# The gate's matrix product over two token groups by seven products, with sums made by accumulating transfers

## Chip, cores and metric

One core of one Trainium2 chip runs the whole program. The time is the device time of one execution in microseconds, the median over runs. All data are f32; the large matmuls split each f32 operand into a rounded part and a rest and add three products of them ("three passes").

## The reference, cut to what matters

```python
mix = jnp.concatenate([y_ssd, y_sc], axis=-1) @ w_out      # 2048 tokens x 2048 @ 2048 x 1024
x = x + rmsnorm(mix, norm_post)
gate = jax.nn.sigmoid(x @ w_ple_gate)                      # 2048 x 1024 @ 1024 x 1024
return x + gate * (p_i @ w_ple_proj)
```

Ahead of these lines stand a normalised input projection, a state space scan and a short convolution; the change leaves them alone but for one scale factor.

## The kernel before

Everything is held transposed: 128 partitions are 128 features, the free dimension is tokens. Tokens come in four groups of 512 (`tg` 0 to 3, `TG` = 512), features in eight tiles of 128 (`d` or `k`, `KD` = 8), so that a tile is 128x512 f32, 256 KB. The input projection (to about 1190 us) already uses a seven product form (`Wino`, line 242): a 2x2 block product by 7 block products instead of 8, with sums of weight halves and of input halves. After the scan come the two stages concerned here, from about 1322 us to the end.

`out_proj(t)` (line 1042) treats token groups t and t+1 together. The half of the output projection that belongs to the convolution was made earlier, beside the scan, and lies in DRAM as `part_d`. A *unit* is one output tile of one group: 24 matmuls (8 k, three passes), into one bank of a PSUM pair (`pss`, 3 pairs of banks; `psm` holds 2 single banks). VectorE adds `part` from PSUM (L1060), ScalarE squares the sum (L1065), VectorE adds the squares up (L1066). There are 32 such units, numbered 0 to 31.

`norm(tg)` (line 1069) sums the squares over partitions by a product with ones (L1072), takes the root (L1074) and the reciprocal over 128x512 (L1075). `residual` (line 1077) multiplies by norm and column (L1081) and adds the input x, loaded as `xres` (L1082). `operands` splits the result for the matmuls (`split_act`, L203 a ScalarE cast, L204 a VectorE difference).

`gate(t)` (line 1089) has again 32 units of 24 matmuls (tiles `mg`), 768 in all; then tanh (L1104), plus one times the projected embedding `pe` (L1105), half of that plus x2 (L1106), and the store. The embeddings' projection `ple_d` is made at the start of the kernel (lines 393 to 402).

Weights come through `Weights` (line 110): pieces of 128x512 in one sequence, loaded to `raw` (9 buffers), cast (L138) and differenced (L139) into one of six slots. `W.next(held)` keeps the slots filled ahead of the matmuls. In `gate` and `out_proj` four pieces are held while both groups use them.

Steps that are not matmuls are hung on units by `after(unit, ...)`, run once the matmuls of that unit are issued. A scheduler then orders each engine's instructions by readiness and by this order; for instance four `mg` matmuls stand ahead of the last `mo` unit in the trace. All transfers are issued on SyncE's queue. `Loads` (line 746) is a pool of three buffers for loads of tile pairs (512 KB).

Of the kernel before, what the change touches and what calls it, by code (L numbers as in the profile page):

```python
# [15 lines left out]
P = 128  # L16
# [39 lines left out]

AHEAD, LATER = (0, 1), (2, 3)
# [3 lines left out]
def hybrid_kernel(ctx: ExitStack, tc: tile.TileContext, xT, pT, w_t, w_dt, w_o, w_g, w_p, cols_d, cst_d, outT):  # L61
# [19 lines left out]
    acs_d = [dram.tile([NH, TB], F32, name=f"acs_d{b}") for b in range(NB)]  # L81

# [24 lines left out]
    def col(i):  # L107
        return cols[:, i:i + 1]
# [253 lines left out]
    with ExitStack() as st:  # L362
# [9 lines left out]
        def first_input():  # L372
# [373 lines left out]
    class Loads:  # L746
# [5 lines left out]
        def begin(self, kind, *at):  # L752
# [3 lines left out]
            if kind in ("mraw", "gn"):  # L756
                b, o = divmod(at[0] * TG, TB)
            if kind == "gn":
                src = grs_d[b][:, o:o + TG].partition_broadcast(P)
            else:  # L760
                if kind == "mraw":
                    k = at[1]
                    src = yz_d[b][k:k + 2, :, o:o + TG] if k < KD else ysc_d[b][k - KD:k - KD + 2, :, o:o + TG]
                elif kind == "part":
                    src = part_d[at[0]][at[1]:at[1] + 2]
                else:
                    src = xT[at[1]:at[1] + 2, :, at[0] * TG:(at[0] + 1) * TG]
                src = src.rearrange("k p t -> p k t")
# [267 lines left out]
    with ExitStack() as st:  # L1036
        pp = st.enter_context(tc.tile_pool(name="pp", bufs=2))
        L3 = Loads(st, "pl3", 3)

        x2s_, ssq_, rs_, sp_ = {}, {}, {}, {}  # L1040

        def out_proj(t):

            for tg in (t, t + 1):
                x2s_[tg] = [None] * KD
                ssq_[tg] = pp.tile([P, TG], F32, tag="ssq", name=f"ssq2_{tg}")
            for dp in range(0, KD, 2):
                sp = []
                for tg in (t, t + 1):
                    x2, ssq = x2s_[tg], ssq_[tg]  # L1050
                    ps = pss.tile([P, 2, TG], F32, tag="ssd", name=f"mo_{tg}_{dp}")
                    pt = L3.get("part", tg, dp)
                    for i in range(2):
                        for q in range(2):
                            if tg == t:
                                sp.append(W.next(len(sp)))
                            mm3([(ps[:, i, :], sp[2 * i + q], acts_o[tg])], 4 * q, 4, KD)
                        d = dp + i
                        x2[d] = pp.tile([P, TG], F32, tag="x2", name=f"x2_{tg}_{d}", bufs=NG * KD)
                        V.tensor_tensor(x2[d], ps[:, i, :], pt[:, i, :], ALU.add)  # L1060
                        if d == 0:
                            S.activation(ssq, x2[d], AF.Square)
                        else:
                            sq = pp.tile([P, TG], F32, tag="sq2", name=f"sq2_{tg}_{d}")
                            S.activation(sq, x2[d], AF.Square)  # L1065
                            V.tensor_tensor(ssq, ssq, sq, ALU.add)  # L1066
                        yield

        def norm(tg):

            ps = mm_bank(f"pn2_{tg}")
            TE.matmul(ps, ones_d, ssq_[tg], start=True, stop=True)  # L1072
            rs = rs_[tg] = pp.tile([P, TG], F32, tag="rs2", name=f"rs2_{tg}")
            S.activation(rs, ps, AF.Sqrt, bias=epsc[:, 0:1])  # L1074
            V.reciprocal(rs, rs)  # L1075

        def residual(tg, d):

            x2, xk = x2s_[tg], L3.get("xres", tg, d)
            for i in range(2):  # L1080
                V.scalar_tensor_tensor(x2[d + i], x2[d + i], col(C_POST + d + i), rs_[tg], ALU.mult, ALU.mult)  # L1081
                V.tensor_tensor(x2[d + i], x2[d + i], xk[:, i, :], ALU.add)  # L1082

        def operands(tg, d):

            for i in range(2):
                sp_.setdefault(tg, []).append(split_act(x2s_[tg][d + i], f"x2s_{tg}_{d + i}", FIRST[2 * (tg % 2) + d // 4]))

        def gate(t):

            for dp in range(0, KD, 2):
                sp = []
                for tg in (t, t + 1):
                    banks = pss.tile([P, 2, TG], F32, tag="ssd", name=f"mg_{tg}_{dp}")
                    for i in range(2):
                        d, ts_, ps = dp + i, slice(tg * TG, (tg + 1) * TG), banks[:, i, :]
                        pe = pp.tile([P, TG], F32, tag="pe", name=f"pe_{tg}_{d}")
                        nc.sync.dma_start(pe, ple_d[tg * TG // TB][d, :, tg * TG % TB:tg * TG % TB + TG])
                        for q in range(2):
                            if tg == t:  # L1100
                                sp.append(W.next(len(sp)))
                            mm3([(ps, sp[2 * i + q], sp_[tg])], 4 * q, 4, KD)
                        th = pp.tile([P, TG], F32, tag="gth", name=f"gth_{tg}_{d}")
                        S.activation(th, ps, AF.Tanh, scale=0.5)  # L1104
                        V.scalar_tensor_tensor(th, th, 1.0, pe, ALU.add, ALU.mult)  # L1105
                        V.scalar_tensor_tensor(th, th, 0.5, x2s_[tg][d], ALU.mult, ALU.add)  # L1106
                        nc.sync.dma_start(outT[d, :, ts_], th)
                        yield

# [6 lines left out]
        def second(tg, at_norm, at_res, at_ops):  # L1116

            after(at_norm, lambda: norm(tg))
            for n, u in enumerate(at_res):
                after(u - 1, lambda d=2 * n: L3.begin("xres", tg, d))  # L1120
                after(u, lambda d=2 * n: residual(tg, d))
            for n, u in enumerate(at_ops):
                after(u, lambda d=2 * n: operands(tg, d))
# [6 lines left out]
        mixes_at(1, -1, -1, 0, 1)  # L1130
        mixes_at(2, 12, 13, 14, 14)
# [8 lines left out]
        for stage in (out_proj, gate):  # L1140
            for t in range(0, NG, 2):
                for _ in stage(t):
                    for step in plan.get(u, ()):
                        step()
                    u += 1

# [61 lines left out]
```

## Time and profile before

| | |
|---|---|
| median of 3 runs | 1699.23 us (1698.92 to 1703.21) |
| profiled execution | 1696.41 us, span 1694.7 us |
| PE, weight load, DVE, ACT, POOL busy | 98%, 80%, 74%, 46%, 3% |
| mean granted TensorE clock | 0.996 |
| transfers | 262.27 MB, 155 GB/s over the span, 46.4% of 16 engines on the one hardware queue |
| output projection (`mo`) | 1322.6 to 1511.9 us |
| gate (`mg`) | 1505.2 to 1689.2 us |

PE is TensorE, DVE VectorE, ACT ScalarE, POOL GpSimd, SP SyncE. The profile gives a group of instructions as line, engine, operation, out<-in by the program's names, and idle time by what ended it. "Landing" of a transfer is the time from its issue to its completion.

### The profile page before, as it was taken

What the parts mean: (1) busy time and instruction counts of PE and PEld (TensorE: products, weight loads), DVE (VectorE), ACT (ScalarE), POOL (GpSimd) and SP (SyncE); (2) the same over time, 40 slices, a digit from 0 to 9 for tenths busy, and PEclk for the clock granted to TensorE, in tenths of its full rate; (3) what the DMA queues carried; (4) which work ended last, traced back from release to release, by engine and by line L of the source; (5) the groups of instructions that cost most, each with busy time, mean ns of one, the idle gap of its engine ahead of it and who ended that gap; (6) DMA issues with size and microseconds to landing.
All of it is one profiled execution on the core that took longest, in us unless ns stands there. A gap on an engine that the chain in (4) does not pass through costs nothing.

```text
span 1694.7 us, 22635 instructions
## 1 busy us (share of the span) xinstructions
PE 1658.7 (98%) x8324; PEld 1351.9 (80%) x8324; DVE 1255.4 (74%) x1843; ACT 783.5 (46%) x1408; POOL 45.6 (3%) x79
## 2 busy tenths in 40 slices
PE   7999999999999999999999999999999899999998
PEld 5788888888888888888888888778777677788886
DVE  7997777988669867677777685689678748878632
ACT  7763444434337434343444353666575324252421
POOL 0000000000000100100000000000000000000000
PEclk9999999999999999999999999999999999999999
DMA  9462221773226322222222237789887735636422
GB/s 303 162 211 70 97 96 61 257 251 120 69 68 213 130 80 95 78 76 68 106 82 102 73 117 239 245 277 278 261 314 242 243 100 168 197 102 211 149 95 87
DMA packets 122691, 262.27 MB, mean 155 GB/s; under 512 B 17098, under 2 KB 19658, under 8 KB 121556
## 3 DMA queue, kind: packets, MB, share of 16 engines
q1 hardware_dynamic: 122580, 260.83, 46.4%
q8 instruction: 65, 1.06, 0.2%
q14 instruction: 46, 0.38, 0.1%
HBM read 192.45 MB, written 68.33 MB: 154 GB/s over the span
## 4 chain that ended last, share of the span: by engine, by line
PE 85%; DMA 6%; DVE 6%; ACT 2%; issue 1%; SPq 0%; DVEq 0%; ACTq 0%
PE mg L214 10%; PE mo L214 8%; PE os L826 6%; PE py L967 1%; PE A_xs1X L310 1%; PE A_gc6X L310 1%; PE A_gc7X L310 1%; PE A_gb6X L310 1%; PE A_z3X L310 1%; PE A_xs3X L310 1%; PE A_gc5X L310 1%; PE A_z2X L310 1%; PE A_xs2X L310 1%; PE A_gb4X L310 1%; PE A_gc4X L310 1%; PE A_gc3X L310 1%
## 5 line engine op out<-in xcount | busy, mean ns | idle before, releaser
L826 PE MATMUL os<-act_m,ws_os 128*128 128x512 f32 x768 | 186.0, 396 | 2.4 <-ACT po L830 1.7
L214 PE MATMUL mo<-act_m,ws_o 128*128 128x512 f32 x768 | 180.9, 396 | 4.3 <-DVE x L1060 4.3
L214 PEld LDWEIGHTS mo<-act_m,ws_o 128*128 128x128 f32 x768 | 144.1, 189 | 42.1 <-issue 6.1
L214 PE MATMUL mg<-act_x2s,ws_g 128*128 128x512 f32 x768 | 176.8, 391 | 0.7 <-ACT gth L1104 0.7
L826 PEld LDWEIGHTS os<-act_m,ws_os 128*128 128x128 f32 x768 | 141.2, 188 | 37.6 <-issue 6.6
L214 PEld LDWEIGHTS mg<-act_x2s,ws_g 128*128 128x128 f32 x768 | 143.0, 188 | 34.2 <-ACT gth L1104 4.4
L139 DVE TENSOR_TENSOR ws_A_gb<-wr_A_gb,ws_A_gb 128x512 fp32r<-128x512 f32 x96 | 65.8, 686 | 33.0 <-ACT ws_A_gb L138 32.9
L138 ACT CAST ws_A_gc<-wr_A_gc 128x512 fp32r<-128x512 f32 x96 | 59.7, 622 | 57.7 <-PE A_gc5X L310 8.3
L138 ACT CAST ws_A_gb<-wr_A_gb 128x512 fp32r<-128x512 f32 x96 | 59.7, 621 | 51.6 <-PE A_cb0Y L310 4.3
L604 DVE SCALAR_TENSOR_TENSOR xo<-ux,cols,xo 128x1024 f32<-128x1024 f32 x60 | 76.7, 1280 | 6.7 <-ACT xo L600 5.6
L939 ACT ACTIVATE m<-m,adt 128x128 f32<-128x128 f32 x256 | 77.5, 391 | 0.6 <-DMA m<-acs_d 0.5
L139 DVE TENSOR_TENSOR ws_A_gc<-wr_A_gc,ws_A_gc 128x512 fp32r<-128x512 f32 x96 | 66.0, 687 | 14.1 <-ACT ws_A_gc L138 12.8
L1105 DVE SCALAR_TENSOR_TENSOR gth<-gth,pe 128x512 f32<-128x512 f32 x32 | 22.1, 691 | 70.5 <-ACT gth L1104 70.4
L1104 ACT ACTIVATE gth<-mg 128x512 f32<-128x512 f32 x32 | 19.1, 598 | 103.7 <-PE mg L214 103.6
L214 PE MATMUL A_ple<-act_p,ws_p 128*128 128x512 f32 x192 | 48.2, 409 | 9.0 <-ACT ws_p L138 8.1
L942 DVE SCALAR_TENSOR_TENSOR m<-m,gsb 128x1024 f32<-128x1024 f32 x32 | 39.6, 1246 | 19.1 <-ACT m L939 16.8
L214 PEld LDWEIGHTS A_ple<-act_p,ws_p 128*128 128x128 f32 x192 | 37.4, 196 | 18.7 <-ACT ws_p L138 9.0
L139 DVE TENSOR_TENSOR ws_A_z<-wr_A_z,ws_A_z 128x512 fp32r<-128x512 f32 x48 | 32.9, 685 | 25.2 <-ACT ws_A_z L138 25.2
L203 ACT CAST act_m<-mraw 128x512 fp32r<-128x512 f32 x64 | 38.1, 621 | 28.9 <-DVE mraw L785 15.8
L138 ACT CAST ws_A_xs<-wr_A_xs 128x512 fp32r<-128x512 f32 x48 | 29.9, 623 | 44.3 <-issue 11.6
L138 ACT CAST ws_A_z<-wr_A_z 128x512 fp32r<-128x512 f32 x48 | 29.9, 623 | 41.9 <-DVE wr_A_z L187 8.6
L1060 DVE TENSOR_TENSOR x<-mo,part 128x512 f32<-128x512 f32 x32 | 22.0, 686 | 29.3 <-PE mo L214 29.3
(499 smaller groups left out, 3597.7 us busy)
## 6 DMA issues: line engine op xcount, KB each, us to landing
wr_A_gc<-in_w_t_dram SPq DMA_DIRECT2D x64, 256.0 KB, 2.5
wr_A_gb<-in_w_t_dram SPq DMA_DIRECT2D x64, 256.0 KB, 2.8
m<-acs_d SPq DMA_DIRECT2D x32, 512.0 KB, 7.7
ple_d<-A_pe SPq DMA_DIRECT2D x32, 256.0 KB, 5.1
wr_A_xs<-in_w_t_dram SPq DMA_DIRECT2D x32, 256.0 KB, 2.6
ysc_d<-vs SPq DMA_DIRECT2D x16, 512.0 KB, 2.7
wr_A_z<-in_w_t_dram SPq DMA_DIRECT2D x32, 256.0 KB, 3.0
xs_d<-xo SPq DMA_DIRECT2D x16, 512.0 KB, 4.0
```

The source lines that it names most:

```text
L138: S.copy(sp[:, 0, :kn, :], raw[:, :kn, :])
L139: V.tensor_tensor(sp[:, 1, :kn, :], raw[:, :kn, :], sp[:, 0, :kn, :].bitcast(F32), ALU.subtract)
L203: S.copy(a[:, 0, :], src)
L214: TE.matmul(out, sp[:, a, (k0 + k) % 4, :], act[k0 + k][:, b, :], start=k0 + k == 0 and q == 0, stop=k0 + k == n - 1 and q == 2)
L310: TE.matmul(out, sp[:, a, k % 4, :], t[:, b, ts_], start=p in OPENS and k == 0 and q == 0, stop=k == nk - 1 and q == 2, skip_group_check=True)
L604: V.scalar_tensor_tensor(o, u[:, q:q + TB], col(w0 + q), o, ALU.mult, ALU.add)
L826: TE.matmul(ps, sp[:, a, k, :], acts_o[tg][KD + kk][:, b_, :], start=kk == 0 and n == 0, stop=kk == KD - 1 and n == 2)
L939: S.activation(m[:, c, :], m[:, c, :], AF.Exp, bias=nacs[b][:, h, c:c + 1])
L942: V.scalar_tensor_tensor(mf, mf, 1.0, s["gsb"][gr], ALU.min, ALU.mult)
L1060: V.tensor_tensor(x2[d], ps[:, i, :], pt[:, i, :], ALU.add)
L1104: S.activation(th, ps, AF.Tanh, scale=0.5)
L1105: V.scalar_tensor_tensor(th, th, 1.0, pe, ALU.add, ALU.mult)
```

## The change

The gate's product is rewritten as a 2x2 block product: rows are the two halves of the output features (tiles 0 to 3 and 4 to 7), the inner dimension is the two halves of the input features, columns are token groups t and t+1. Seven products p, each of four output tiles n and four k tiles: 12 matmuls for each (p, n). A gate unit is now 12 matmuls; there are 28 for t = 0 (units 32 to 59) and 28 for t = 2 (units 60 to 87). Each has a weight piece of its own. Products 1, 6, 7 and 4 accumulate in bank X of their tile, 5 and 3 in another, 2 in a third; three of them (1, 5, 6) are copied out half-way (`kept`), and a finished tile is such a copy plus a bank (for product 4 the bank alone).

Four sums of weight halves per tile n are formed on VectorE during the output projection and stored to `sg_d` (`gate_sums`), then loaded as pieces. Operand sums are made on VectorE in place (`operand`: three for product 6, one for product 7).

Three additions move from VectorE to transfers that add into SBUF, issued by GpSimd: the stored half `part_d` into the copied bank (16 of 512 KB), the residual x (16 of 512 KB), and, for all but the last four tiles, x2 into the gated embedding (28 of 256 KB). For this last addition x2 is stored (`kept`, 16 stores of 512 KB, three or four units after the residual's transfer), since `operand` overwrites it. An output store stands three units after its accumulating transfer.

The norm takes four single-column products, root and reciprocal over 128x4, and spreads the result by a diagonal and a second product. The factor 0.5 of the gate moves to the embeddings' projection (`S.mul`, same instruction count).

```diff
+GORDER = (1, 2, 6, 5, 3, 7, 4)
+GATES = ([(p, n) for p in (1, 2, 6) for n in range(4)]
+         + [(p, n) for h in (0, 2) for p in (5, 3) for n in (h, h + 1)]
+         + [(p, n) for p in (7, 4) for n in range(4)])
...
+    def gate_piece(p, n):
+        if p in (1, 2, 4):
+            return w_g[n + 4 * int(p == 4), :, 4 * int(p != 1):4 * int(p != 1) + 4, :]
+        return sg_d[n][{5: 0, 6: 1, 7: 2, 3: 3}[p]]
...
-        seq += [direct(w_g[d, :, 4 * q:4 * q + 4, :], f"g{t}_{d}_{q}", praw) for d in range(KD) for q in (0, 1)]
+        seq += [direct(gate_piece(p, n), f"g{t}_{p}_{n}", praw) for p, n in GATES]
...
-                        S.copy(pe, ps)
+                        S.mul(pe, ps, 0.5)
...
-                        V.tensor_tensor(x2[d], ps[:, i, :], pt[:, i, :], ALU.add)
+                        S.copy(x[:, i, :], ps[:, i, :])
+                        if i == 1:
+                            G.dma_start(x, rows(part_d[tg][dp:dp + 2]), accum_op=ALU.add)
+                            unit = 8 * t + 2 * dp + 2 * (tg - t) + i
+                            lag = 4 if unit == 31 else 2
+                            after(unit + lag, lambda tg=tg, d=dp: squares(tg, d))
+                            after(unit + lag + 1, lambda tg=tg, d=dp: squares(tg, d + 1))
...
+            def sums():
+                ssq = ssq_[tg]
+                ps = mm_bank(f"pn2_{tg}")
+                for c in range(TG // P):
+                    TE.matmul(ps[:, c:c + 1], ssq[:, c * P:(c + 1) * P], ones_d[:, 0:1], start=True, stop=True)
+                q = const.tile([P, TG // P], F32, tag="rq2", name=f"rq2_{tg}")
+                S.activation(q, ps[:, 0:TG // P], AF.Sqrt, bias=epsc[:, 0:1])
+                V.reciprocal(q, q)
+                V.tensor_tensor(ssq.rearrange("p (c t) -> p c t", t=P), ident.unsqueeze(1).to_broadcast([P, TG // P, P]),
+                                q.unsqueeze(2).to_broadcast([P, TG // P, P]), ALU.mult)
+
+            def spread():
+                ps = mm_bank(f"prs2_{tg}")
+                TE.matmul(ps, ones_d, ssq_[tg], start=True, stop=True)
+                rs = rs_[tg] = pp.tile([P, TG], F32, tag="rs2", name=f"rs2_{tg}")
+                S.mul(rs, ps, float(D))
...
-                V.tensor_tensor(x2[d + i], x2[d + i], xk[:, i, :], ALU.add)
+            G.dma_start(x2s_[tg][d // 2], rows(xT[d:d + 2, :, tg * TG:(tg + 1) * TG]), accum_op=ALU.add)
+
+        def kept(tg, d):
+            nc.sync.dma_start(rows(x2_d[tg][d:d + 2]), x2s_[tg][d // 2])
...
+            a, b, c, d = w
+            V.tensor_tensor(d, c, d, ALU.add)
+            V.tensor_tensor(c, c, a, ALU.subtract)
+            V.tensor_tensor(a, a, d, ALU.subtract)
+            V.tensor_tensor(b, b, a, ALU.add)
...
+            if p == 6:
+                src = tmp(f"t2_{t}{k}")
+                V.tensor_tensor(b11, b12, b11, ALU.subtract)
+                V.tensor_tensor(src, b11, b22, ALU.subtract)
+                V.tensor_tensor(b21, b21, src, ALU.add)
+            elif p == 7:
+                src = b12
+                V.tensor_tensor(b12, b12, b22, ALU.subtract)
+            else:
+                src = {1: b11, 2: b21, 5: b11, 3: b22, 4: b21}[p]
...
+                V.scalar_tensor_tensor(th, th, 1.0, L.get("pe", tg, d - d % 2)[:, d % 2, :], ALU.add, ALU.mult)
+                store = lambda: nc.sync.dma_start(outT[d, :, tg * TG:(tg + 1) * TG], th)
+                if last and p == 4:
+                    V.tensor_tensor(th, th, L.get("x2", tg, d - d % 2)[:, d % 2, :], ALU.add)
+                    store()
+                else:
+                    G.dma_start(th, x2_d[tg][d], accum_op=ALU.add)
+                    after(unit + 3, store)
...
+                out, sp = bank[BANK[p], n], W.next()
+                for k in range(4):
+                    for q, (a, b) in enumerate(PASSES):
+                        TE.matmul(out, sp[:, a, k, :], ops_[t, p][k][:, b, :], start=p in OPENS and k == 0 and q == 0,
+                                  stop=k == 3 and q == 2, skip_group_check=True)
+                if p in (1, 5, 6):
+                    keep[p, n] = tmp(f"kp_{t}_{p}{n}")
+                    S.copy(keep[p, n], out)
+                else:
+                    finish(p, *at(p, n), out, keep.get(({2: 1, 3: 6, 7: 5, 4: 0}[p], n)), unit)
...
-        second(0, 16, (19, 20, 21, 22), (29, 29, 30, 30))
-        second(1, 18, (24, 25, 26, 27), (31, 31, 32, 32))
-        second(2, 32, (35, 36, 37, 38), (45, 45, 46, 46))
-        second(3, 34, (40, 41, 42, 43), (47, 47, 48, 48))
+        second(0, 17, (19, 20, 21, 22), 3)
+        second(1, 19, (23, 24, 25, 26), 3)
+        operands_at(0, 29, 30)
+        operands_at(1, 30, 31)
+        operands_at(2, 32, 33, 34, 35)
+        second(2, 33, (37, 39, 41, 43), 4)
+        operands_at(3, 36, 37)
+        second(3, 38, (45, 47, 49, 51), 4)
...
```

More of the change, by code (lines that the diff above doesn't have):

```diff
@@ L81, in hybrid_kernel @@
     acs_d = [dram.tile([NH, TB], F32, name=f"acs_d{b}") for b in range(NB)]
+    sg_d = [dram.tile([4, P, 4, P], F32, name=f"sg_d{n}") for n in range(KD // 2)]
+    x2_d = [dram.tile([KD, P, TG], F32, name=f"x2_d{g}") for g in range(NG)]
     cols = const.tile([P, NCOL], F32, name="cols")
@@ L755, in begin @@
             t = self.ready[(kind, *at)] = self.pool.tile([P, 2, TG], F32, tag="ld", name="_".join(map(str, (kind, *at))))
-            if kind in ("mraw", "gn"):
-                b, o = divmod(at[0] * TG, TB)
+            b, o = divmod(at[0] * TG, TB)
             if kind == "gn":
@@ L763, in begin @@
                     src = yz_d[b][k:k + 2, :, o:o + TG] if k < KD else ysc_d[b][k - KD:k - KD + 2, :, o:o + TG]
-                elif kind == "part":
-                    src = part_d[at[0]][at[1]:at[1] + 2]
+                elif kind == "pe":
+                    src = ple_d[b][at[1]:at[1] + 2, :, o:o + TG]
                 else:
-                    src = xT[at[1]:at[1] + 2, :, at[0] * TG:(at[0] + 1) * TG]
+                    src = x2_d[at[0]][at[1]:at[1] + 2]
                 src = src.rearrange("k p t -> p k t")
@@ L1037, in hybrid_kernel, with after, tmp, x2 @@
         pp = st.enter_context(tc.tile_pool(name="pp", bufs=2))
-        L3 = Loads(st, "pl3", 3)
-        x2s_, ssq_, rs_, sp_ = {}, {}, {}, {}
+        x2s_, ssq_, rs_, ops_ = {}, {}, {}, {}
+        plan = {}
+        def after(unit, *steps):
+            plan.setdefault(unit, []).extend(steps)
+        def tmp(name):
+            return pp.tile([P, TG], F32, tag="kp", name=name, bufs=11)
+        def x2(tg, d):
+            return x2s_[tg][d // 2][:, d % 2, :]
+        def rows(a):
+            return a.rearrange("k p t -> p k t")
+        def squares(tg, d):
+            ssq = ssq_[tg]
+            if d == 0:
+                S.activation(ssq, x2(tg, d), AF.Square)
+            else:
+                sq = pp.tile([P, TG], F32, tag="sq2", name=f"sq2_{tg}_{d}")
+                S.activation(sq, x2(tg, d), AF.Square)
+                V.tensor_tensor(ssq, ssq, sq, ALU.add)
         def out_proj(t):
             for tg in (t, t + 1):
-                x2s_[tg] = [None] * KD
+                x2s_[tg] = []
                 ssq_[tg] = pp.tile([P, TG], F32, tag="ssq", name=f"ssq2_{tg}")
@@ L1057, in out_proj @@
                             mm3([(ps[:, i, :], sp[2 * i + q], acts_o[tg])], 4 * q, 4, KD)
[L1058 to L1066, printed above, removed]
@@ new lines, in out_proj, with norm @@
+                        yield
+        def norm(tg, unit):
+            def sums():
+                ssq = ssq_[tg]
+                ps = mm_bank(f"pn2_{tg}")
[11 more added lines that the diff above has]
+                S.mul(rs, ps, float(D))
+            after(unit, sums)
+            after(unit + 1, spread)
@@ L1077, in residual @@
         def residual(tg, d):
-            x2, xk = x2s_[tg], L3.get("xres", tg, d)
             for i in range(2):
[L1081 to L1087, printed above, removed]
-        def gate(t):
[L1091 to L1108, printed above, removed]
@@ L1111, in hybrid_kernel @@
-        plan = {}
-        def after(unit, *steps):
-            plan.setdefault(unit, []).extend(steps)
-        def second(tg, at_norm, at_res, at_ops):
-            after(at_norm, lambda: norm(tg))
+                V.scalar_tensor_tensor(x2(tg, d + i), x2(tg, d + i), col(C_POST + d + i), rs_[tg], ALU.mult, ALU.mult)
+            G.dma_start(x2s_[tg][d // 2], rows(xT[d:d + 2, :, tg * TG:(tg + 1) * TG]), accum_op=ALU.add)
+        def kept(tg, d):
+            nc.sync.dma_start(rows(x2_d[tg][d:d + 2]), x2s_[tg][d // 2])
@@ L1119, in second, with operands_at @@
+        def second(tg, at_norm, at_res, lag):
+            norm(tg, at_norm)
             for n, u in enumerate(at_res):
-                after(u - 1, lambda d=2 * n: L3.begin("xres", tg, d))
                 after(u, lambda d=2 * n: residual(tg, d))
-            for n, u in enumerate(at_ops):
-                after(u, lambda d=2 * n: operands(tg, d))
+                after(u + lag, lambda d=2 * n: kept(tg, d))
+        def operands_at(g, *units):
+            for k in range(4):
+                after(units[k * len(units) // 4], lambda k=k: operand(g, k))
@@ L1145, in hybrid_kernel @@
                     u += 1
+        for v in sorted(plan):
+            if v >= u:
+                for step in plan[v]:
+                    step()
 _OUTS = [((KD, P, T), 'float32')]
```

68 lines of the change are left out of this document (60 added, 8 removed).

## The prediction

> **What bounds the kernel now.** I read the summary of the page first (busy shares), then the chain that ended last, then the stretch around the change (output projection and gate) by the chain in order of time, by windows and by engine timelines.
>
> ```profile
> span 1694.7 us, 22635 instructions
> PE 1658.7 (98%) x8324; PEld 1351.9 (80%) x8324; DVE 1255.4 (74%) x1843; ACT 783.5 (46%) x1408; POOL 45.6 (3%) x79
> PE 85%; DMA 6%; DVE 6%; ACT 2%; issue 1%; SPq 0%; DVEq 0%; ACTq 0%
> ```
>
> TensorE is busy 98% of the span and carries 85% of the chain: a matmul removed is worth its own pitch as long as nothing else takes its place. The end of the chain in order of time (start, length, what):
>
> ```profile
> 1505.37 0.91 PE mg L214 x4
> 1506.28 5.65 PE mo L214 x24
> 1511.93 4.54 PE mg L214 x20
> 1516.46 0.86 PE pn L1072 x2
> 1517.32 10.89 PE mg L214 x48
> 1528.22 0.86 PE pn L1072 x2
> 1529.08 153.69 PE mg L214 x672
> 1682.79 0.61 ACT gth L1104
> 1683.43 5.75 PE mg L214 x24
> 1689.20 0.61 ACT gth L1104
> 1689.84 0.70 DVE gth L1105
> 1690.56 0.69 DVE gth L1106
> ```
>
> The gate's 768 matmuls (mg) take 0.91+4.54+10.89+153.69+5.75 = 175.8 us, 0.229 us each, with one gap of 0.6 us. Who keeps TensorE waiting from 1320 us to the end (total, times, longest), and what the other engines do in the gate and before it:
>
> ```profile
> PE pn L230 <- DVE ssum L977: 4.7, 2, 3.8
> PE mo L214 <- DVE x L1060: 4.3, 4, 1.7
> PE mg L214 <- ACT gth L1104: 0.7, 1, 0.7
> ...
> 1360.00:1380.00 20.00, 20.00 (x89) 16.12 (x87) 7.52 (x11) 4.39 (x7) 0.00 (x0) 1.00 0.39 116
> ...
> 1440.00:1460.00 20.00, 20.00 (x90) 16.55 (x89) 19.89 (x31) 4.77 (x8) 0.00 (x0) 1.00 0.66 209
> 1529.10:1682.80 153.70, 153.65 (x672) 124.84 (x671) 82.39 (x124) 42.58 (x72) 0.00 (x0) 1.00 0.42 141
> ```
>
> Columns after the length: PE, weight load, DVE, ACT, POOL busy (instructions), clock, DMA share, GB/s. In the gate PE never rests, VectorE works 82 of 154 us, ScalarE 43, the DMA engines 42%. So the gate is bound by matmuls alone, and VectorE is full only around 1440 us.
>
> **The change, part by part.**
>
> *Seven products for eight.* Per pair of token groups 7 products x 4 output tiles x 12 matmuls = 336 instead of 384: 672 in all, 96 fewer, 96 x 0.229 = **-22.0 us**. The 672-matmul piece above shows that count at full pace: 153.7 us.
>
> *Weights for one use each.* A piece serves 12 matmuls instead of 24: 56 pieces instead of 32, each a cast (ACT) and a difference (DVE). With the operands (14 sets of four instead of 32 tiles), kept products and first differences, VectorE's load in the gate grows. Its price per instruction, when it never rests:
>
> ```profile
> 1550.05 1.41 DVE L1081 SCALAR_TENSOR_TENSOR x<-x,cols,rs 128x512 f32<-128x512 f32 x2
> 1551.38 0.68 DVE L1082 TENSOR_TENSOR x<-x,xres 128x512 f32<-128x512 f32 x1
> 1551.98 0.68 DVE L1105 SCALAR_TENSOR_TENSOR gth<-gth,pe 128x512 f32<-128x512 f32 x1
> 1552.58 0.68 DVE L139 TENSOR_TENSOR ws_g<-wr_g,ws_g 128x512 fp32r<-128x512 f32 x1
> ```
>
> Starts are 0.60 us apart (0.665 for the one with a column), though each is reported as 0.68. First half of the gate (28 units of 12 matmuls, 28 x 2.745 = 76.8 us): 28 weight differences, 60 operand instructions (16 each for the two sets of product 6 prepared there, 8 for one product 7, five sets of 4), 28 to finish tiles, 4 sums of squares = 120 x 0.60 = 72, plus 16 norm products x 0.665 = 10.6 and 2 for the norms: **85 us for 77**. Second half: 23+20+32 = 75 x 0.60 = 45 us for 77. So VectorE falls about 8 us behind by the end of the first half and recovers in the second. The cover is the prefetch: six weight slots, a piece is split five units (13.7 us) ahead, so 8 us of lag reaches nothing. Without overlap (0.686 and 0.745 as reported) it would be 96 us, 19 behind, 5 us past that cover. ScalarE in the first half: 28 casts of weights, 32 of operands, 28 evacuations, 4 squares at about 0.62, and 5 us of table loads = 62 of 77: hidden.
>
> *Norm.* Before, each norm is one product with ones (0.86 us, the pn rows). Now four single-column products and one full one. The nearest row is a run of 16 records with 16 columns (a product in f32 leaves two):
>
> ```profile
> 280.67 1.95 PE L535 MATMUL A_pdt<-cst,dtT 32*128 32x16 f32 x16
> ...
> L214 PEld LDWEIGHTS mg<-act_x2s,ws_g 128*128 128x128 f32 x768 | 143.0, 188 | 34.2 <-ACT gth L1104 4.4
> ```
>
> 0.12 us a record, eight records more per norm: 4 x 1.0 = **+3.9 us** on PE (0 if they fall into gaps, 6 if each of the 32 records takes a whole weight load of 188 ns); the first row, the same kind of small f32 product, is nearest. The reciprocal shrinks from 512 columns to 4:
>
> ```profile
> 1427.15 3.35 DVE L1075 RECIPROCAL rs<-rs 128x512 f32<-128x512 f32 x1
> 1471.72 0.69 DVE L1082 TENSOR_TENSOR x<-x,xres 128x512 f32<-128x512 f32 x1 [2.01 <-DMA xres<-in_xT_dram]
> 1354.88 1.42 DVE L785 SCALAR_TENSOR_TENSOR mraw<-mraw,cols,gn 128x512 f32<-128x512 f32 x2 [2.74 <-DMA mraw<-yz_d]
> ```
>
> *Output projection.* 32 adds of the stored part and 32 residual adds leave VectorE; PSUM is emptied by 32 ScalarE copies. The four PE waits on L1060 (4.3 us) come where VectorE stands in a reciprocal, waits for xres (row 1471.72) or for mraw (row 1354.88). The first two causes go; the mraw wait stays, since ScalarE's casts queue behind the same load. I take **-2.6 us** of the 4.3 (bounds 0 and -4.3). Late next is the sum of squares, which now waits for an accumulating transfer; it stands two units (11 us) behind its issue. The stored halves cost 16 VectorE instructions (9.6 us) and 32 transfers of 256 KB in units 1 to 13, where VectorE is busy 7.5 of 20 us and the DMA engines 0.39 (row 1360): hidden.
>
> *Accumulating transfers and the DMA load.* Nothing in the trace accumulates and POOL issues no transfer. The nearest rows (KB, us to landing), and windows in which the DMA engines are saturated:
>
> ```profile
> xres<-in_xT_dram SPq DMA_DIRECT2D x16, 512.0 KB, 4.2
> pe<-ple_d SPq DMA_DIRECT2D x32, 256.0 KB, 2.8
> part<-part_d SPq DMA_DIRECT2D x16, 512.0 KB, 5.8
> ...
> 24.00:32.00 8.00, 8.00 (x37) 6.61 (x36) 7.22 (x14) 7.70 (x16) 0.00 (x0) 1.00 1.05 391
> 1160.00:1168.00 8.00, 7.55 (x41) 5.66 (x41) 7.26 (x9) 7.89 (x25) 0.00 (x0) 1.00 1.01 379
> ```
>
> In units 36 to 59 (66 us at full pace) the queues carry, in tiles of 0.262 MB: 24 weights, 14 embeddings, 16 last sums, 13 outputs, 16 residuals of groups 2 and 3, 16 stores of the finished x2: 99, 26 MB, 394 GB/s; the row of 24 us shows 391. So copies alone just fit, with nothing to spare. If an accumulate occupies the engines twice (it must read its destination too), 32 tiles more make 34.3 MB, 88 us at 391 GB/s. A price below a copy's is excluded, since the same bytes move; above, nothing in the trace bounds it, and I take the pe and xres rows as nearest. On the SP queue an output store waits for its accumulate, three units (8 us) after the matmuls, and weight loads, embeddings and stores stand behind it; the cover is that raw weights run up to nine buffers ahead:
>
> ```profile
> SPq L134 <- DVE ws_g L139: 25.3, 18, 4.1
> ```
>
> (SP already waits for a raw buffer to come free, not the reverse.) For lags of VectorE and transfers together I put **+4 us** on PE, between 0 and the rivals below.
>
> The Trainium skill (DMA: Bandwidth & Descriptors, Specifications) gives a core some 358 GB/s of HBM; the 391 of the row above is more, so here the measurement decides, but by the page's figure the 26 MB would need 72.5 us, an estimate 6.5 us beyond the 66, most of it inside the prefetch.
>
> *End.* Tanh, two VectorE instructions, store: as in the last three rows of the chain, 0.
>
> Sum: -22.0 + 3.9 - 2.6 + 4.0 = -16.7. The profiled execution took 1696.4 us (span 1694.7 and 1.7 around it), which is 2.8 under the median of 1699.23: 1679.7 for such an execution, 1682.5 at the median.
>
> **Rivals.**
>
> *A: the accumulates cost the DMA engines twice a copy.* 88 us of transfers in 66; of the 22 us excess the look-ahead of embeddings and weights covers about four units, 11 us; the other 11 hold up VectorE, then the banks, then PE. 1682.5 + 11 - 2 (half of the 4 us of lag is then in it already) = 1691. For it: the window is full already with plain copies. Against: the gate's second half asks only 76 tiles in 77 us, 259 GB/s, so some traffic can slide there.
>
> *B: VectorE is the bound in the first half.* If its instructions do not overlap (96 us) and each of 12 finishing additions waits 0.75 us for its tanh (9 us), 105 us for 77, 28 behind less 13.7 cover: 14 instead of 4, 1693. Against: rows 1551 to 1552, where other work stands between the two steps.
>
> *C, slower than before: accumulates run one at a time.* If POOL's queue works off one transfer before the next (or POOL needs that long to issue it), units 36 to 51 hold 8 of 256 KB and 8 of 512 KB, 24 tiles in 44 us. The gain is used up when the delay reaches 17 us plus 11 of cover, that is at 72 us or 3.0 us per 256 KB. Rows stand just under: 2.8 alone, 2.1 for half of an xres. At double those prices, 5 us a tile, 120 us in 44: 1682.5 + 76 - 11 = 1748. Half-way, at 4 us, 1724. For it: no row of POOL issuing a transfer. Against: SP's transfers overlap freely.
>
> *D: no change.* The product form saves its matmuls for certain; only together with A and B in part (16 us of waits) would nothing be left, 1699.
>
> **How the numbers follow.** Forecast 0.56; A 0.16; B 0.10; C 0.11; D 0.07. A measurement of this kernel tells 0.3% (5.1 us) from no change. Faster than 1694.1: the forecast, most of A and half of B, 0.74; within: D and the rest of A and B, 0.14; slower: C and a little of D, 0.12. The forecast's own range is 1674 (no lag, 4.3 won, columns in gaps: 1699.2 - 22.0 - 4.3) to 1690. The range for eight in ten leaves out C's far end: 1673 to 1704.
>
> **What would show it.** mg with 672 matmuls, about 154 us plus gaps; mo's wait on L1060's place under 2 us; the new f32 columns near 1 us a norm; VectorE nearly full from unit 36 to 59; DMA share near 1 there. The prediction is wrong if accumulate landings exceed about 8 us, if PE waits in the gate on VectorE or ScalarE total more than 10 us, or if SP waits for accumulates with raw weights run out behind it.

## The result, and the profile after

The changed kernel takes 1834.65 us (median of 6 runs, 1830.06 to 1846.75); the kernel before, in the same comparison, 1699.08 us (1693.78 to 1703.21). Ratio 1.0809 [1.0782, 1.0837]: 8% slower, where 1682.5 was forecast. The profiled execution was the slowest of the six, 1846.75 us. Its page: span, busy time by engine, the two DMA queues (packets, MB, share of 16 engines' span; q1 is SyncE's queue, q0 GpSimd's, all of it transfers that add):

```profile
span 1845.1 us, 22915 instructions
PE 1676.7 (91%) x8260; PEld 1362.1 (74%) x8260; DVE 1262.7 (68%) x1875; ACT 834.4 (45%) x1514; POOL 109.2 (6%) x139
q1 hardware_dynamic: 126580, 268.17, 44.1%
q0 software_dynamic: 12736, 24.12, 8.0%
PE 70%; issue 14%; DMA 8%; DVE 3%; POOL 2%; ACT 2%; SPq 0%; POOLq 0%; ACTq 0%; DVEq 0%
```

The 64 matmul records fewer (96 of the gate, less 32 that the norm adds) are there, yet TensorE is busy longer than before (1676.7 for 1658.7 us), and its share of the chain falls from 85 to 70%. The waits of TensorE from 1300 us on (total, times, longest):

```profile
PE mo L223 <- ACT x L1096: 88.8, 14, 29.1
PE mg_X L1215 <- DVE kp L1182: 33.7, 2, 22.5
PE mg_X L1215 <- ACT gth L1180: 3.2, 2, 2.5
PE prs L1121 <- DVE ssq L1116: 3.0, 1, 3.0
```

So 89 us are lost in the output projection (L1096 is the copy that empties a bank), and 34 in the gate in two waits, 11.2 and 22.5. What those engines wait for in turn, all engines and SyncE's queue:

```profile
POOL x L1098 <- ACT x L1096: 190.9, 13, 19.2
ACT sq L1076 <- DMA x<-part_d: 121.8, 14, 31.4
DVE kp L1184 <- DMA pe<-ple_d: 23.1, 1, 23.1
SPq L1135 <- DMA x<-in_xT_dram: 112.0, 16, 13.7
SPq L1185 <- DMA kp<-x_d: 58.8, 19, 11.8
```

ScalarE waits 122 us for stored halves to be added before it can square, and TensorE waits for ScalarE. In the gate VectorE waits 23 us for an embedding, which is the longer of TensorE's two waits; for what ends the shorter one the profile names no engine. The landings, to set beside xres 4.2 and pe 2.8 of before (KB, us):

```profile
x<-part_d POOLq DMA_DIRECT2D x16, 512.0 KB, 7.0
x<-in_xT_dram POOLq DMA_DIRECT2D x16, 512.0 KB, 7.5
kp<-x_d POOLq DMA_DIRECT2D x24, 256.0 KB, 6.6
```

Two things make this. First, GpSimd's timeline (start, busy, idle before and its releaser):

```profile
1524.85 1.22 POOL L1132 DMA_DIRECT2D x<-in_xT_dram  x1 [5.18 <-DVE x L1131]
1531.93 1.21 POOL L1132 DMA_DIRECT2D x<-in_xT_dram  x1 [5.86 <-issue]
1539.05 1.22 POOL L1132 DMA_DIRECT2D x<-in_xT_dram  x1 [5.92 <-issue]
1546.80 1.21 POOL L1132 DMA_DIRECT2D x<-in_xT_dram  x1 [6.53 <-issue]
1553.49 1.22 POOL L1098 DMA_DIRECT2D x<-part_d  x1 [5.47 <-issue]
```

Issues stand 6.7 to 7.8 us apart, about as long as a landing, with idle time that ends on "issue": nothing that the profile shows holds the engine, and still the next transfer is issued only about when the last has landed. The last row shows the damage: a stored half stands in line behind residuals, and TensorE's wait of 29.1 us, which ends at 1562, belongs to it. Second, ScalarE's timeline in the output projection, and the chain there:

```profile
1388.58 0.63 ACT L1076 ACTIVATE sq<-x 128x512 f32<-128x512 f32 x1 [9.54 <-DMA x<-part_d]
1389.11 0.57 ACT L1096 COPY x<-mo 128x512 f32<-128x512 f32 x1
```

```profile
1376.60 0.59 ACT x L1096
...
1377.55 10.93 DMA x<-part_d
...
1388.58 0.09 ACT sq L1076
...
1389.11 0.58 ACT x L1096
...
1389.73 7.18 PE mo L223 x24
```

The square of one tile stands on ScalarE ahead of the next copy out of PSUM. It waits for its transfer, the copy waits behind it, and the next 24 matmuls wait for the copy. One more cost follows from the waits: windows (columns as in the prediction) around TensorE's idle stretch from 1722.0 to 1744.5 us.

```profile
1726.00:1727.00 1.00, 0.00 (x0) 0.00 (x0) 0.00 (x0) 0.00 (x0) 0.00 (x0) 1.00 1.06 182
1728.00:1729.00 1.00, 0.00 (x0) 0.00 (x0) 0.00 (x0) 0.00 (x0) 0.00 (x0) 0.50 0.45 78
1746.00:1747.00 1.00, 1.00 (x4) 0.81 (x3) 0.23 (x1) 0.08 (x1) 0.36 (x1) 0.50 1.09 356
1748.00:1749.00 1.00, 1.00 (x6) 0.82 (x5) 0.00 (x0) 0.00 (x0) 0.00 (x0) 1.00 1.05 318
```

The granted clock falls from 1.00 to 0.50 between 5 and 6 us after the last matmul, and is back at 1.00 some 3 us after the first new one (between 1747 and 1748 us). Over the output projection a matmul is reported at 428 ns for 396 before, 202.7 us for 180.9 in all. The Trainium skill (TensorE: Matmul & The Clock Gate, What's actually happening) says that the array runs at half its clock after at least one idle window of about 3.4 us, and at full clock after about 3.4 us of work; the steps to 0.50 and back agree with that.

### The profile page after: what moved, and what is told of

It is laid out like the page before. It is cut to its first block, busy times and chain, and to the rows that moved or that the text cites. A ratio compares the mean times of both kernels' runs of the same rounds, so it can differ in the third digit from the quotient of the medians.

```text
span 1845.1 us, 22915 instructions
## 1 busy us (share of the span) xinstructions
PE 1676.7 (91%) x8260; PEld 1362.1 (74%) x8260; DVE 1262.7 (68%) x1875; ACT 834.4 (45%) x1514; POOL 109.2 (6%) x139
## 3 DMA queue, kind: packets, MB, share of 16 engines
q1 hardware_dynamic: 126580, 268.17, 44.1%
q0 software_dynamic: 12736, 24.12, 8.0%
## 4 chain that ended last, share of the span: by engine, by line
PE 70%; issue 14%; DMA 8%; DVE 3%; POOL 2%; ACT 2%; SPq 0%; POOLq 0%; ACTq 0%; DVEq 0%
PE os L840 6%; PE mo L223 3%; DMA x<-part_d 3%; PE mg_Y L1215 2%; PE A_ple L223 2%; PE mg_X L1215 1%; PE A_xs1X L319 1%; PE A_gc6X L319 1%; PE A_gb5X L319 1%; PE A_gc7X L319 1%; PE A_gb6X L319 1%; PE A_cb0X L319 1%; PE A_gc1X L319 1%; PE A_z2X L319 1%; PE A_gc2X L319 1%
## 5 line engine op out<-in xcount | busy, mean ns | idle before, releaser
L223 PE MATMUL mo<-act_m,ws_o 128*128 128x512 f32 x768 | 202.7, 428 | 88.8 <-ACT x L1096 88.8
L223 PEld LDWEIGHTS mo<-act_m,ws_o 128*128 128x128 f32 x768 | 159.7, 210 | 133.6 <-ACT x L1096 95.2
L1215 PE MATMUL mg_X<-act_x2s,ws_g 128*128 128x512 f32 x384 | 97.7, 413 | 36.9 <-DVE kp L1182 33.7
L1215 PEld LDWEIGHTS mg_X<-act_x2s,ws_g 128*128 128x128 f32 x384 | 74.9, 198 | 57.7 <-DVE kp L1182 35.1
L1077 DVE TENSOR_TENSOR ssq<-ssq,sq 128x512 f32<-128x512 f32 x28 | 19.3, 688 | 91.4 <-ACT sq L1076 91.4
L148 DVE TENSOR_TENSOR ws_A_gc<-wr_A_gc,ws_A_gc 128x512 fp32r<-128x512 f32 x96 | 66.2, 689 | 13.8 <-ACT ws_A_gc L147 12.5
L1076 ACT ACTIVATE sq<-x 128x512 f32<-128x512 f32 x28 | 17.5, 630 | 121.8 <-DMA x<-part_d 121.8
L1215 PE MATMUL mg_Y<-act_x2s,ws_g 128*128 128x512 f32 x288 | 67.4, 392 | 0.0
L1215 PEld LDWEIGHTS mg_Y<-act_x2s,ws_g 128*128 128x128 f32 x288 | 53.6, 188 | 12.5 <-ACT kp L1219 0.8
L148 DVE TENSOR_TENSOR ws_o<-wr_o,ws_o 128x512 fp32r<-128x512 f32 x32 | 22.0, 690 | 58.3 <-ACT ws_o L147 58.2
L148 DVE TENSOR_TENSOR ws_g<-wr_g,ws_g 128x512 fp32r<-128x512 f32 x56 | 38.6, 688 | 17.3 <-ACT ws_g L147 14.2
```

Of the source, the lines that this page charges most:

```text
L148: V.tensor_tensor(sp[:, 1, :kn, :], raw[:, :kn, :], sp[:, 0, :kn, :].bitcast(F32), ALU.subtract)
L223: TE.matmul(out, sp[:, a, (k0 + k) % 4, :], act[k0 + k][:, b, :], start=k0 + k == 0 and q == 0, stop=k0 + k == n - 1 and q == 2)
L1076: S.activation(sq, x2(tg, d), AF.Square)
L1215: TE.matmul(out, sp[:, a, k, :], ops_[t, p][k][:, b, :], start=p in OPENS and k == 0 and q == 0, stop=k == 3 and q == 2, skip_group_check= ...
```

## The experiments

Theory 1: GpSimd's queue has room for one 512 KB adding transfer at a time (both kernels set `dynamic_dma_scratch_size=1024`), so they run one after the other. Theory 2: the squares' place on ScalarE passes each delay on to TensorE. They may add up; the rivals are that one of them does it all, or theory 3, the transfers' price in the DMA engines, or a fourth, the seven product form itself. Theories 4 and 5 came up on the way: 4, the order on SyncE's queue makes embeddings late; 5, adding transfers take the DMA engines' time twice (theory 3 again, for what is left in the gate). In plain and half_order_plain the additions are left out, so their results are not the kernel's; they show times only. Since the output projection begins between 1321 and 1334 us in these profiles whatever is edited behind it, the table also gives the time from its first matmul to the end of the span.

| kernel | median us | ratio to before, 95% | first `mo` to end |
|---|---|---|---|
| before (medians of four comparisons) | 1696.4 to 1699.1 | 1 | 372.1 |
| changed | 1834.65 | 1.0809 [1.0782, 1.0837] | 510.8 |
| ring1280 | 1783.66 | 1.0501 [1.0469, 1.0533] | 461.1 |
| half | 1757.32 | 1.0347 [1.0317, 1.0377] | 432.6 |
| order | 1767.51 | 1.0396 [1.0356, 1.0437] | 438.2 |
| half_order | 1712.53 | 1.0086 [1.0060, 1.0113] | 384.7 |
| half_order_ring | 1702.58 | 1.0025 [1.0014, 1.0036] | 377.2 |
| half_order_late | 1711.62 | 1.0067 [1.0042, 1.0091] | 388.0 |
| none_acc | 1704.12 | 1.0040 [1.0022, 1.0058] | 377.1 |
| part_dve_half | 1699.22 | 1.0013 [0.9997, 1.0029] | 374.6 |
| plain | 1706.62 | 1.0061 [1.0042, 1.0080] | 381.1 |
| half_order_plain | 1683.55 | 0.9920 [0.9904, 0.9936] | 353.0 |
| res_half | 1704.74 | 1.0054 [1.0035, 1.0073] | 377.2 |
| last_only | 1716.91 | 1.0111 [1.0094, 1.0128] | 388.7 |

### Room on the queue: ring1280 and half

```diff
-    nc = _bacc.Bacc("TRN2", ..., dynamic_dma_scratch_size=1024)
+    nc = _bacc.Bacc("TRN2", ..., dynamic_dma_scratch_size=1280)
```

> Only the room for GpSimd's transfer descriptors grows, from 1024 to 1280 bytes of each partition. Theory 1 (one at a time): in the profile of the changed kernel GpSimd issues a 512 KB accumulating transfer only when the one before has landed, every 6.5 to 7.5 us, because the room holds one; with a quarter more it holds two. Then the long waits of TensorE behind such queues (12.0 and 29.1 us in the output projection, 11.2 and 22.5 us in the gate, 75 us) mostly go: 1770 us, 1755 to 1785. Theory 2 (order: ScalarE stands in a sum of squares that waits for its accumulate, and the next PSUM copy stands behind it): the 14 shorter waits of 3 to 8 us stay whatever the room. Theory 3 (price: an accumulate occupies the DMA engines twice as long per byte, and they are the limit): 1835 us, within 8.

51 us of the 136 (1834.65 less 1699.08) come back from one number. Residuals on GpSimd's timeline:

```profile
1502.20 1.22 POOL L1132 DMA_DIRECT2D x<-in_xT_dram  x1 [4.25 <-DVE x L1131]
1506.17 1.21 POOL L1132 DMA_DIRECT2D x<-in_xT_dram  x1 [2.74 <-issue]
1510.16 1.21 POOL L1132 DMA_DIRECT2D x<-in_xT_dram  x1 [2.77 <-issue]
```

They now stand 4.0 us apart and land in 8.8 (median): two are in flight. No wait and no order of the program was changed, so the room for descriptors was the limit. TensorE's wait in the output projection falls from 88.8 to 63.9 us and its longest from 29.1 to 11.7, and in the gate from 33.7 to 13.8.

```diff
-    G.dma_start(x, rows(part_d[tg][dp:dp + 2]), accum_op=ALU.add)
+    [G.dma_start(x[:, j, :], part_d[tg][dp + j], accum_op=ALU.add) for j in range(2)]
-    G.dma_start(x2s_[tg][d // 2], rows(xT[d:d + 2, :, ...]), accum_op=ALU.add)
+    [G.dma_start(x2(tg, d + j), xT[d + j, :, ...], accum_op=ALU.add) for j in range(2)]
```

> Each 512 KB accumulating transfer is issued as two of 256 KB, same bytes, same room for descriptors. Theory 1: three of 256 KB were seen issued back to back, so more bytes are in flight: as with more room, 1765 us (1750 to 1790), and issues of 0.9 us each show in GpSimd's row. Theory 2: the short waits in the output projection stay, 47 us of them. Theory 3: 1835 us or a little more, since bytes and packets are the same.

The same bytes in pieces that fit beside each other: 77 us back. A stored half lands in 4.2 us per 256 KB. In ring1280 14 waits stay in the output projection, in half 15 (44.8 us in all), as theory 2 said of them.

What fills the room seems to go by the packets on q0 (the expectations count descriptors, which no view shows). By the counts of the runs an adding transfer of 512 KB has 272 packets and one of 256 KB 144 (13248 / 92 in half); a plain copy of 512 KB has 144 and one of 256 KB 80 (7360 / 92 in half_order_plain). In the same 1024 bytes GpSimd issued three of 144 packets one after the other, adding ones in the changed kernel and copies in plain, where one of 272 ran alone:

```profile
1729.59 2.67 POOL L1190 DMA_DIRECT2D kp<-x_d  x3 [6.92 <-issue]
```

### The place of the squares: order, and both together

```diff
-    S.activation(sq, x2(tg, d), AF.Square)
+    a = S.activation(sq, x2(tg, d), AF.Square)
+    tc.add_manual_dep(a.ins, newest[0].ins.name, NOSYNC, ...)   # newest[0]: the last copy out of PSUM
```

> Only the order on ScalarE is changed: a sum of squares may not stand ahead of the copy of the newest unit issued before it, so that it comes two units behind its accumulate as the plan says. Theory 2: the waits of 3 to 8 us between pairs of units (47 us, and some 10 us of slower clock behind them) go, the four long ones stay: 1780 us, 1765 to 1795. Theory 1 alone: the copy is not what waits, 1835 us within 8.

> The two edits together: accumulating transfers of 256 KB, and sums of squares behind the newest PSUM copy on ScalarE. Theories 1 and 2 are separate causes: of the 44.8 us of TensorE's waits on the PSUM copy that halving left (15 waits, the longest 7.0), nearly all go, with some slow clock behind them; the wait of 13.5 us in the gate and the longer end stay: 1707 us (1698 to 1722). If both edits had only relieved the same queue (one cause): not under 1740 us.

With the squares behind the newest copy alone, the output projection's 14 waits become 4:

```profile
PE mo L223 <- ACT x L1099: 41.5, 4, 29.8
```

The short ones go, 47 of the 89 us, and the long ones, of transfers in line, stay. The time, 1767.5, came out 12 us under the forecast of 1780. Together the two edits bring 1712.5, 122 of 136 us; alone they bring 77 and 67, so some 22 us are in both: a transfer that lands sooner also holds a badly placed square for less. What is left of TensorE's waits in half_order:

```profile
PE mg_X L1218 <- DVE kp L1185: 14.3, 1, 14.3
PE mo L223 <- ACT x L1099: 8.2, 3, 4.9
```

> As the run before, and 1280 bytes for descriptors. Theory 1 as it stands (a 256 KB accumulate takes a little over 16 of 64 descriptors per engine, so three were in flight, now four): a little less, 1703 us (1695 to 1718). If three in flight already fill the DMA engines: the same as the run before within 3 us.

More room on top takes the `mo` wait to 3.4 and the time to 1702.6; in the gate 13.0 us of wait on VectorE stay.

### The 14 us in the gate: half_order_late, plain, half_order_plain

In half_order VectorE stands 14.8 us for an embedding (`pe<-ple_d`), loaded on SyncE's queue. Theory 4 blamed the queue's order: stores that wait for adding transfers stand ahead of that load.

```diff
-    nc.sync.dma_start(rows(x2_d[tg][d:d + 2]), x2s_[tg][d // 2])
+    behind_load(nc.sync.dma_start(rows(x2_d[tg][d:d + 2]), x2s_[tg][d // 2]))   # output stores likewise
-    ... (37, 39, 41, 43), 4) ... (45, 47, 49, 51), 4)    # lag of the stores of groups 2 and 3
+    ... (37, 39, 41, 43), 8) ... (45, 47, 49, 51), 8)
```

> As the first of this group, and on SyncE's queue the stores that wait for an accumulate (x2 kept, outputs) stand behind the newest load of embeddings, x2's stores eight units after the residual instead of four. Theory 4 (SyncE's order: in the gate VectorE waits 12.8 us for embeddings whose load stands behind a store of x2 that waits for its accumulate): the 13.5 us wait of TensorE in the gate goes: 10 us less than the first of this group, about 1697 us. If the load is late for bandwidth: no less than 3 us.

The expectation of theory 4 was missed: 1711.6, no better, and the wait in the gate grew to 21.3 us. But the run does not refute the theory. SyncE's queue in half_order_late (wait, then timeline):

```profile
SPq L1191 <- DMA kp<-x_d: 14.1, 1, 14.1
1594.01 0.34 SPq L1191 DMA_DIRECT2D out_dram<-kp  x1
1594.45 0.39 SPq L783 DMA_DIRECT2D pe<-ple_d  x1
```

The late load still stands right behind an output store that waits for its adding transfer (in half_order too: store at 1598.36, load at 1598.80), since the edit puts a store behind the newest load before it, not behind the next one. And the stores of x2, now later, hold up VectorE in their turn, which may overwrite x2 only when it is stored: 11.5 us (`x_d<-x`) beside 9.8 for the embedding. The windows of half_order show another thing:

```profile
1560.00:1610.00 50.00, 37.07 (x161) 29.48 (x159) 34.18 (x56) 20.58 (x37) 16.30 (x19) 0.92 1.08 283
```

The DMA engines are full (1.08) for 50 us, while they move only 283 GB/s, where nearly the same share (1.05) meant 391 in the kernel before. Hence theory 5, tried by taking out the addition alone, in the changed kernel (plain) and in half_order (half_order_plain), and leaving the transfers, their sizes, queue and waits:

```diff
-    G.dma_start(..., accum_op=ALU.add)     # all three kinds
+    G.dma_start(...)
```

> The changed kernel with its three kinds of GpSimd transfers left as plain copies (the additions of the stored half, of x and of x2 are left out; same sizes, queue and waits). Theory 1 (room for descriptors, and a transfer that adds needs about twice of it and twice the engines' time): landings fall from 7.0 to 4 to 5 us, two go at a time, q0's share falls from 0.33 to about 0.17% per MB, time 1700 to 1750. Rival (the issue on GpSimd's queue serialises whatever the transfer does): landings stay above 6 us with one at a time and the time stays above 1800.

> half_order (256 KB transfers, squares ordered behind the newest copy) with plain copies in place of the transfers that add (the additions are left out). In half_order the DMA engines are full from 1560 to 1610 us (share 1.08) while they move 283 GB/s, and the gate waits 14 us on a late embedding. Theory 5 (the transfers that add take the engines' time twice, so the queue of SyncE's loads runs late): share below 1, the gate's wait on VectorE under 4 us, time 1686 to 1696. Rival (order on SyncE's queue: loads stand behind stores that wait): the gate's wait stays at 10 us or more, time 1705 to 1713.

half_order_plain takes 1683.55 us, 29 less than half_order and 2.5 under the range that theory 5 gave. Its queues, TensorE's waits, and windows in the gate:

```profile
q1 hardware_dynamic: 126580, 268.17, 48.1%
q0 software_dynamic: 7360, 24.12, 4.3%
```

```profile
PE mg_X L1218 <- ACT gth L1183: 1.4, 2, 0.7
PE mo L223 <- ACT x L1099: 1.1, 1, 1.1
```

```profile
1560.00:1580.00 20.00, 20.00 (x90) 16.42 (x89) 19.44 (x33) 12.24 (x22) 4.85 (x9) 1.00 1.04 402
1580.00:1600.00 20.00, 19.30 (x85) 15.52 (x84) 18.99 (x32) 12.51 (x23) 3.69 (x7) 1.00 1.05 401
```

The engines are as full as before, but move 402 GB/s, and no wait of TensorE in the gate is longer than 0.7 us. Per MB, q0 takes 4.3/24.12 = 0.18% of the span, like q1 (48.1/268.17 = 0.18); in the changed kernel it took 8.0/24.12 = 0.33 against 0.16. With the spans, 1683.6 and 1845.1 us, that is 3.0 us of all 16 engines per MB for a copy, and 6.1 for an adding transfer. So an adding transfer occupies the engines twice as long per byte, with nearly twice the packets (12736 for 6848 in plain, the same transfers). The share of 1.04 and more falls short of what theory 5 expected (below 1); the wait went all the same: at 402 GB/s the loads keep up.

That the additions cost these 29 us is shown; by which path is not. Taking them out also frees room (half_order_ring, with more room alone, gets 10 of the 29), and it shortens what SyncE's stores of x2 wait for, between 1560 and 1600 us in half_order and then in half_order_plain:

```profile
SPq L1138 <- DMA x<-in_xT_dram: 23.5, 7, 5.7
SPq L1138 <- DMA x<-in_xT_dram: 5.4, 3, 2.4
```

So theory 5 may well work through theory 4's queue; no run holds the one and frees the other.

plain keeps the 512 KB pieces and the squares' old place, and still takes only 1706.62 us: under the changed kernel's own waits and order the addition costs 128 us. On GpSimd's timeline and in the landings:

```profile
1582.28 0.72 POOL L1132 DMA_DIRECT2D x<-in_xT_dram  x1 [2.49 <-DVE x L1131]
1583.61 0.73 POOL L1132 DMA_DIRECT2D x<-in_xT_dram  x1 [0.60 <-DMA x_d<-x]
```

```profile
x<-part_d POOLq DMA_DIRECT2D x16, 512.0 KB, 4.5
x<-in_xT_dram POOLq DMA_DIRECT2D x16, 512.0 KB, 7.3
```

Copies are issued 1.3 us apart, with landings of 7.3: several are in flight in the same room. The landings were expected at 4 to 5 us; the stored half's came to 4.5, but the residual's copies landed no sooner than adding transfers (7.5). So the loss lies not in one transfer's landing, but in how many go at once and in the engines' time. An issue takes 0.72 us of GpSimd for 1.22. The rival, that GpSimd's issue serialises whatever the transfer does, is out. What plain still loses to half_order_plain, 23 us, stands mostly in 21.2 us of `mo` waits, 13 of up to 4 us: the squares' place and the 512 KB pieces together, small once landings are short.

The Trainium skill (DMA: Bandwidth & Descriptors, SWDGE vs HWDGE vs iDMA) says that a transfer that adds can only come from GpSimd, whose software writes a pair of descriptors per operation into rings in SBUF before data move. The runs fit that (room in SBUF as the limit, issue time that goes with the packets); the doubling they add to it.

### The additions back on VectorE, in whole or in part

In none_acc VectorE does all three additions, with plain loads (one buffer for x, two gated tiles fewer); the seven products and the rest stay.

```diff
-    S.copy(x[:, i, :], ps[:, i, :]) ... G.dma_start(x, ..., accum_op=ALU.add)
+    V.tensor_tensor(x[:, i, :], ps[:, i, :], pt[i], ALU.add)
-    G.dma_start(x2s_[tg][d // 2], rows(xT[...]), accum_op=ALU.add)
+    V.tensor_tensor(x2(tg, d + i), x2(tg, d + i), xk[:, i, :], ALU.add)
-    G.dma_start(th, x2_d[tg][d], accum_op=ALU.add)
+    V.tensor_tensor(th, th, L.get("x2", tg, d - d % 2)[:, d % 2, :], ALU.add)
```

> All three additions go back to VectorE with plain loads (stored half, residual, x2 of every tile); the seven product form, its stored sums, operands, norm and weights stay; nine instead of eleven buffers for temporaries and one buffer for the residual's loads. Theories 1 to 3 all put the loss on the accumulating transfers: 1690 us, 1678 to 1706 (VectorE then has some 104 us of work for the 77 us of the gate's first half). Rival 4 (the seven product form itself is the trouble, by its weights' splits or its PSUM banks): over 1740 us.

1704.12, 0.4% slower than before. A window of its gate:

```profile
1580.00:1600.00 20.00, 11.49 (x41) 8.84 (x41) 19.42 (x33) 5.36 (x9) 0.00 (x0) 0.83 0.88 298
```

VectorE is full while TensorE has 11.5 us of work in 20. From the last `mo` matmul to the gate's last it takes 177 us (1513.1 to 1690.4), as before (1511.9 to 1689.2): what the product form saves is lost again. TensorE waits 14 us in the gate, 11 of them for VectorE, and the clock is lower around the waits (0.83 in this window). VectorE in turn stands 19 us for loads of x2, x and embeddings from 1500 us on. So rival B shows here, in another kernel than the one it was named for, but mixed with late loads; how much is VectorE's own work was not told apart.

Three kernels take parts of this diff: part_dve_half its first pair of lines (the stored half by VectorE; the residual by transfers of 256 KB as in half, and the last sum by transfers); res_half the first and the third; last_only the first and the second.

> One accumulate undone alone: the stored half of the output projection is loaded and added by VectorE as before; the residual accumulates in transfers of 256 KB, the last sum as in the change. ScalarE then waits for no transfer in the output projection: theory 2 gives the same relief there as the order edit, less VectorE's 32 additions in a stage where it has room: 1702 us (1692 to 1716), with the wait in the gate still there. If the residual's accumulates alone cost as much (theory 1 for them): over 1730 us.

> Only the residual is added by transfers, of 256 KB; the stored half and gate's last sum by VectorE with plain loads. Theory 5: 24 of part_dve_half's 56 adding transfers go, the 12 of them in the full stretch take 3.1 MB x 0.17% = 0.5% of the span, 9 us of engine time, off it; VectorE gets 12 more adds (7 us) there. The gate's wait on VectorE falls from 15 to 4 to 10 us, time 1688 to 1700. Rival (order on the queue): no change from 1699 or slower, as loads of x2 come on SyncE's queue.

> Only gate's last sum is added by transfers (256 KB); the stored half and the residual by VectorE with plain loads (a buffer for the loads of x more, two gated tiles fewer). Theory 5: 12 to 14 adding transfers in the first gate half instead of 28, so the engines are full later; VectorE has 16 adds (10 us) more there and is near full, as in none_acc. Time 1692 to 1706, PE's waits in the gate 6 to 14 us. Rival (order on the queue): as part_dve_half, 1699 to 1710, with the wait on a late embedding of 10 us or more.

part_dve_half is the best kernel that leaves no addition out, 1699.22, the same as before. It has half_order's wait, with the same signs (13.9 us on VectorE, ending at 1604; 11.9 us of VectorE for an embedding; DMA share 1.08 to 1.10 from 1560 to 1600). Both others took longer than theory 5 expected. In res_half the wait only falls to 11.1, for an expected 4 to 10, and the time is 0.5% over before: VectorE now waits 23.1 us for its loads of x2 (`x<-x_d`). That is what the rival, the order on SyncE's queue, gave for it (1699 or slower). In last_only it waits 14.6 us for x (`xres`) and TensorE loses 8.0 us in the output projection. Fewer adding transfers alone did not pay: plain loads took their place, and these were waited for. Whether these loads come late by the three load buffers or by full DMA engines (shares 0.93 to 1.08 in res_half from 1540 to 1600) was not told apart.

## Why the prediction was wrong

**The failed step: adding transfers priced as copies.** "I take the pe and xres rows as nearest" put them at 2.8 us per 256 KB and 4.2 per 512, and took them to overlap. They landed in 6.6 and 7.0 to 7.5 us, took the engines 6.1 us per MB for a copy's 3.0, and 512 KB of them left no room for a second. The landing alone was not the step: the nearest rows were too low for copies of this stage too (5.4 and 7.3 us in plain). The +4 us of lags became 37 us of waits in the gate, plus 89 in the output projection, where the prediction held the transfers covered.

half_order_plain is the kernel that the sum described, with copies in place of the adding transfers and squares out of the way: 1683.55, where 1682.5 was forecast. That these are 1 us apart is partly luck. The kernel before had a median of 1696.7 in that comparison, so the gain by medians is 13.1 us for 16.7 forecast; from the first `mo` to the end it is 19.1 (372.1 to 353.0). And two terms missed in opposite ways: lags 1.4 us for 4, end 3.3 us for 0.

**A second failed step: "it stands two units (11 us) behind its issue."** The lag was written in the program's order, but the scheduler put the square ahead of the next copy. With copies that and the 512 KB pieces cost 23 us together (plain against half_order_plain); with adding transfers, order gives back 67 us.

**Rivals.** C had the mechanism, one at a time, and its break-even of 3.0 us per 256 KB was passed at 3.5 (7.0 for 512 KB). Its size was wrong twice over: it counted 24 tiles of units 36 to 51, while 16 transfers of the output projection did most of the harm, through ScalarE; and the last sum's pieces of 256 KB did not run one at a time, but landed in 6.6 us, not in half of 7.0. Its price of 1724 at 4 us stands against 1834.65. Its chance of 0.11 rested on "SP's transfers overlap freely", a row of another queue. A's price was right (0.33 for 0.16% per MB, twice). Its size was not: the wait in the gate is 14 us for A's 11, but the additions cost half_order 29 us in all, where A put 1691 for 1682.5. B shows in none_acc, in part.

**What held.** The matmuls: in half_order_plain the gate's 672 take about 156 us (0.233 each, from the stretch of 1515.4 to 1674.8 less norms and gaps), 19 less than before, for 22 forecast: they stand 0.233 us apart, not 0.229. A norm's eight small records:

```profile
1521.18 0.94 PE L1115 MATMUL pn<-ones_d,ssq 128*128 128x1 f32 x8
```

That is near the 1.0 forecast. The `mo` wait falls by 3.2 us, from 4.3 to 1.1 (2.6 forecast). VectorE is nearly full, as forecast: 19.4 and 19.0 of 20 us busy in the two windows above, with TensorE idle for 0.7 us. The plain copies fit, as forecast: 402 GB/s moved for the 394 asked. The end was not 0 but 3.3 us (last matmul at 1674.8, span 1683.6; before 1689.2 and 1694.7): the last load of x2 comes late, issued on SyncE's queue right behind an output store that waits for its GpSimd transfer.

**The signs it named.** That "accumulate landings exceed about 8 us" did not show at the medians (6.6 to 7.5), only in single ones (10.9 in the chain above); "PE waits in the gate on VectorE or ScalarE total more than 10 us" did (37 us), and SyncE waited 171 us for adding transfers, though what ran out behind it were embeddings, not raw weights. The output projection was missing from the list but for its "wait under 2 us".

## What to carry to other kernels

A transfer that adds is not a copy: count it twice in the DMA engines' time (6.1 us per MB for 3.0 here), look at how many fit into the descriptor room of the queue that issues it, and cut it small enough for more than one. When an engine's work is handed to a transfer, look at who reads the result and at what stands behind that reader on its queue: squares of 0.6 us each, one place too early on ScalarE, were worth 47 of the 89 us that TensorE lost in the output projection. And where a price has no row of its kind, a large change should keep a way back for that part alone: of the kernels here that leave no addition out, none was faster than the one before.

## What the runs showed of the hardware that was not expected

- The room for descriptors decides how many transfers of GpSimd's queue run: with the setting at 1024 one adding transfer of 512 KB (272 packets, some 7 us apart), at 1280 two (4.0 us apart, landing 8.8); at 1024 three of 144 packets were issued in a row.
- An adding transfer takes the DMA engines 6.1 us per MB for a copy's 3.0 (8.0% of 1845.1 us and 4.3% of 1683.6 us for 24.12 MB), and GpSimd 1.22 us to issue 512 KB for a copy's 0.72.
- With copies alone 402 GB/s were moved over 20 us, at a share of 1.04. The Trainium skill (DMA: Bandwidth & Descriptors, Specifications) states some 358 GB/s for a core, from which the prediction worked out its estimate of 72.5 us; the 402 are above that again, with one core running, and the measurement decides.
